# A hybrid attention layer on one core: wider units in the narrow split job, GpSimd's position sums four units ahead, head transposes one tick earlier, and the third query tile beside the first two

## The chip, the cores and the metric

The kernel runs on one core of a Trainium2 chip. The time is the device time of the whole program in microseconds (us); before the change it is 1510.8 us, the median of three runs (1509.91 to 1511.21). The profile is one further execution.

## What is computed

```python
h  = x @ w_in                                    # 512x2048 by 2048x11808, columns q, k, v, z, gates, ...
y_a = (fox(fq, fk, fv, ff + b_f) * silu(fz)) @ w_a   # 8 heads, causal, forget-gate bias
y_b = (nsa(nq, ..., gates) * silu(nz)) @ w_b         # 8 heads, 2 groups; compressed, selected, window branch
out = layer_norm(ALPHA * x + (sigmoid(ga) * y_a + sigmoid(gb) * y_b) @ w_o)
# the compressed branch: blocks of 32 raw keys (values), stride 16, plus a position table, through a two-layer MLP
blocks = raw[:, blk_idx] + pos
k_cmp  = gelu(blocks.reshape(..., 32 * 128) @ w1) @ w2
```

All is float32 and 512 rows long.

## The kernel before

**Units.** The program is one list `units` of pieces of TensorE work. Most need a piece of a weight matrix, which comes by a DMA on SyncE's queue into one of three buffers `wr` (`load`, L159; a chunk is two pieces) and is split into a high and a low part that TensorE multiplies in fp32r: ScalarE copies the high part `wh` (L96), VectorE subtracts for the low part `wl` (L97). A product is three matmuls (`mm3`, L105; `mm_two`, L111). `stream` emits, for unit n, first the split of unit n+3 (`split_w(n + AHEAD)`), then the matmuls of unit n; `wh` and `wl` have four buffers each, so a split can run only when the unit four before it has been multiplied. After the split of a chunk's second half the load of the chunk three further on is issued.

**Ticks.** Attention runs as generators beside the units. Every `tick()` (two 128-row pieces of a projection, six matmuls) advances them by one step: first `active`, then the queue `tq` of second halves of heads (`fox_t`, `nsa_t`), then `sq` of first halves (`fox_s`, `nsa_s`). A FoX head's first half multiplies q by k for four row blocks (`s<-k,q`), takes the exponentials (VectorE L376, ScalarE L378) and normalises the rows (VectorE L387). Its second half transposes them (TensorE L396, out `pt`, two PSUM banks), splits the transposes (`pT`, L96 and L97) and multiplies by v. A transpose of the third step needs the bank whose split was made for the first. All engines work through their instructions in the order emitted.

**Narrow job.** `pairs` computes six column groups of w_in with seven products on half matrices, of eight row tiles of 128 each; T4, T1 and so on name the products. Their right sides are chunks (`wr`) or sums held in `s` and `r`, some made by accumulating DMAs on GpSimd's queue (L979). Five jobs are 512 columns wide; the second, for NSA's values, is 256 wide. One unit is one row tile: six matmuls.

**Position sums.** The compression's first layer is cut in 32 units (`cmp_units`), 16 for keys at heads 1 and 2 and 16 for values at heads 4 and 5, two of them after every two projection units. Each needs four sums of raw keys or values and a position column on GpSimd (L799, `af`), emitted with the unit's split; ScalarE and VectorE then split them (`a<-af`). GpSimd also loads and masks the heads' bias rows (`cbr`, L458, and `cbx`, L462).

**Fill.** `y_fill` multiplies FoX's output by two column groups of w_a beside the last NSA head: eight weight tiles for query tiles 0 and 1, six matmuls each with one tick; then, from the weights kept, tile 2 and tile 3 in units of two weight tiles (`more`). PSUM banks turn over d, d, m.

Of the kernel before, what the change touches and what calls it, by code (L numbers as in the profile page):

```python
# [13 lines left out]
F32R = mybir.dt.float32r  # L14
# [11 lines left out]
H = 8  # L26
# [36 lines left out]
def layer(ctx, tc, x, w_in, b_f, pos_k, pos_v, wk1, wk2, wv1, wv2, w_a, w_b, w_o, ln_g, ln_b, rel, onehot, out):  # L63
# [101 lines left out]
    def split_w(n):  # L165
        while pos["split"] <= min(n, len(units) - 1):
            u = units[pos["split"]]
            pos["split"] += 1
            if "before" in u:
                u["before"]()  # L170
            if "late" in u:
                src = u["late"]()
            elif "chunk" in u:
                w = u.get("width", UW)
                src = chunks[u["chunk"]]["raw"][:, u["half"] * w:(u["half"] + 1) * w]
            else:
                continue
            if "into" in u:
                hi, lo = u["into"]()
            else:  # L180
                hi = base.tile([P, UW], F32R, name="wh", tag="wh", bufs=AHEAD + 1)[:, :src.shape[-1]]
                lo = base.tile([P, UW], F32R, name="wl", tag="wl", bufs=AHEAD + 1)[:, :src.shape[-1]]
            split(hi, lo, src)
            u["w"] = (hi, lo)
            if "prep" in u:
                u["prep"](u)
            if "after" in u:
                u["after"](u)
            if "chunk" in u:
                load(u["chunk"] + 2 + u["half"])  # L190

    def number_chunks():
        for u in units:
# [249 lines left out]
    def fox_t(h, st):  # L443
        key = ("f", h)
        yield from wait_for(("p", key), ("v", key), ("z", key))
        if h < H - 1:
            yield
        yield from take_later("o")
        o = bank("o", 1)
        items = [dict(j=j, p=st["p"], tag=st["tag"], v=vt[key], o=o, first=j == 0, last=j == NT - 1) for j in range(NT)]  # L450
        yield from staged(items, (tr_p, split_p, None, pv))
        gate_out(key, h, o)
        done.add(("t", key))
# [316 lines left out]
    def cmp_units(kv, l00):  # L770

        w = wk1 if kv == "k" else wv1
        at = len(units)

        def pe(u, half):
            l0 = l00 + LB * half
            hi, lo = (t.rearrange("p (l n) -> p l n", l=LB) for t in u["w"])
            a = u["a"]
            n = G * NCMP
            if l0 == 0:  # L780
                assert kv == "k" or ("cmp", "k") in done, "the bank is still in use"
                hid[kv] = bank("m", 1)
            o = hid[kv][:, :CMP_HID]
            for l in range(LB):
                mm_two(o, n, a[:, l], hi[:, l], lo[:, l], l0 + l == 0, l0 + l == CMP_LEN - 1)
            if half:
                tick()
            if l0 + LB == CMP_LEN:
                active.append(cmp_finish(kv))

        def prep(u):
            af = small("af", P, LB * G * NCMP).rearrange("p (l g c) -> p l g c", l=LB, g=G)
            a = pool("fox").tile([P, LB, 2 * G * NCMP], F32R, name="a", tag="a", bufs=AHEAD + 1)
# [7 lines left out]
            split(a[:, :, :n], a[:, :, n:], af.rearrange("p l g c -> p l (g c)"))  # L801
            u["a"] = a

        add_chunk(lambda r: r.rearrange("p (l n) -> p l n", n=CMP_HID),
                  dram(w, l00 * P * CMP_HID, [[CMP_HID, P], [P * CMP_HID, 2 * LB], [1, CMP_HID]]), pe, prep=prep)
        new = units[at:]
        del units[at:]
        return new
# [128 lines left out]
    def pairs(jobs, ops, kh, ent):  # L937
# [24 lines left out]
        def one(j, w, ncols, r0, cols, width, evac):  # L962
# [71 lines left out]
            def out12(width=width, cols=cols, evac=evac):  # L1034
                for i in range(HT):
                    evac(HT + i, cols[0], st[1][i][:, :width], None)


            for op, acc, fresh, quad, after, post in (
                    ("T4", 3, True, (1, 1), first_sum, no_post), ("T1", 1, True, "s", None, keep5),  # L1040
                    ("B11", 0, True, (0, 0), both_sums, keep1), ("T2", 2, True, "s", "sum4", mix),
                    ("B21", 0, False, (1, 0), None, out11), ("T3", 2, False, "r", "rest", out2),
                    ("B22", 1, False, "s", None, out12)):
                for k in range(kh):
                    def pe(u, op=op, acc=acc, fresh=fresh, k=k, post=post, width=width):
                        if fresh and k == 0:
# [10 lines left out]
                    u = {"pe": pe, "width": width}  # L1057
                    if after == "rest":
                        u["after"] = lambda u, k=k, follows=follows: load_rest(k, follows, 1)
                    elif after == "sum4":  # L1060
                        u["after"] = lambda u, k=k: sum4(u, k)
                    elif after is not None and k % 2:
                        u["after"] = lambda u, k=k, after=after: after(k, chunks[u["chunk"]])
                    if quad in ("s", "r"):
                        u["late"] = lambda k=k, quad=quad, width=width: st[quad][:, k, :width]
                    else:
                        u["half"] = k % 2
                        if k % 2 == 0:
                            u["view"] = lambda r, width=width: r[:, :2 * width].rearrange("p (k c) -> p k c", k=2)
                            u["src"] = rows(jobs[j], quad[0] * kh + k, quad[1])  # L1070
                    units.append(u)
            if j == 0:
                units[-7 * kh]["before"] = open_all

        for j, job in enumerate(jobs):
            one(j, *job)
# [199 lines left out]
    def y_fill(n):  # L1276

        st = {}

        def next_bank():  # L1280
            t = fin["turn"] = (fin.get("turn", -1) + 1) % 3
# [8 lines left out]
        def pe(u, kt):  # L1290
            st["w", kt] = u["w"]
            for i in range(2):
                if kt == 0:
                    st[i] = next_bank()
                y_mm(st[i], i, 0, kt, u["w"])
            tick()
            if kt == H - 1:
                gate(0)
                gate(1)

        def more(i, kt):
            def f(u):
                if kt == 0:
# [330 lines left out]
```

## Time and profile before

| | |
|---|---|
| median of three runs | 1510.8 us |
| profiled execution | 1510.6 us |
| its span, first to last instruction | 1508.6 us |
| granted TensorE clock, mean | 0.997 of full |
| TensorE busy | 1488.4 us, 99% |
| VectorE, ScalarE, GpSimd busy | 864.8, 663.0, 221.9 us |

Busy is the time in which an engine has at least one instruction in it; matmuls overlap, so a busy TensorE can still run slowly. The list of waits says for an engine's line what it waited for: total us, times, longest. In a timeline a row is a start in us, a duration, engine, line, operation, out<-in and, in brackets, the idle time before it and what ended it; like rows that touch are merged, so a row can stand for several instructions (x4).

### The profile page before, as it was taken

The page shows a single profiled execution, that of the slowest core. Times are in us where ns is not written, and L with a number is a line of the kernel's source. Part 1 is how long each engine was busy: PE and PEld are TensorE (multiplying, and loading weights), DVE is VectorE, ACT ScalarE, POOL GpSimd, SP SyncE. Part 2 cuts the span into 40 slices and gives each one's busy share as a digit, 9 for nine tenths or more (in the row PEclk, how much of TensorE's full clock was granted, in tenths as well). Part 3 has the DMA queues.
Part 4 walks back from the last instruction along what each step waited for, and adds up shares of the span by engine and source line. Part 5 has one row for each costly group of instructions (what it writes and reads, how often), then busy time and mean ns, then how long its engine had stood idle before and what let it go on. Part 6 is the DMA issues. An engine that isn't in the chain of part 4 may idle for free.

```text
span 1508.6 us, 19701 instructions
## 1 busy us (share of the span) xinstructions
PE 1488.4 (99%) x7081; PEld 1232.6 (82%) x7081; DVE 864.8 (57%) x1721; ACT 663.0 (44%) x1300; POOL 221.9 (15%) x363
## 2 busy tenths in 40 slices
PE   8999999999999999999999999999999999999998
PEld 6788898888888888788787888888887888888886
DVE  4666667676767646645544456646675344444455
ACT  6255665656565535435433344434453222222233
POOL 1211112020101046224230000000000100030001
PEclk9999999999999999999999999999999999999999
DMA  8678578687877564434542332233332433373336
GB/s 228 160 227 194 140 196 196 187 198 192 195 195 190 146 195 147 133 92 129 144 111 77 105 91 71 59 86 93 87 100 85 144 121 122 113 243 98 126 112 167
DMA packets 192176, 214.87 MB, mean 142 GB/s; under 512 B 13024, under 2 KB 127760, under 8 KB 192080
## 3 DMA queue, kind: packets, MB, share of 16 engines
q1 hardware_dynamic: 168688, 159.93, 35.3%
q0 software_dynamic: 23104, 53.18, 16.1%
q8 instruction: 55, 0.90, 0.2%
q10 hardware_dynamic: 288, 0.52, 0.1%
q14 instruction: 41, 0.34, 0.1%
HBM read 195.96 MB, written 21.27 MB: 144 GB/s over the span
## 4 chain that ended last, share of the span: by engine, by line
PE 87%; issue 5%; POOL 3%; DMA 2%; DVE 2%; ACT 1%; SPq 0%; POOLq 0%; ACTq 0%
PE d L105 42%; PE s L105 15%; PE pt L105 9%; PE o L105 9%; PE m L105 8%; POOL af L799 2%; PE pt L396 1%; DMA cbr<-negc_d 1%; DMA wr<-in_w_in_dram 1%; DVE wl L97 1%; PE o L111 0%; POOL cbx L462 0%; PE m L111 0%; PE d L1240 0%; ACT xs L96 0%
## 5 line engine op out<-in xcount | busy, mean ns | idle before, releaser
L97 DVE TENSOR_TENSOR wl<-wr,wh 128x512 fp32r<-128x512 f32 (+1 forms) x476 | 320.9, 681 | 307.4 <-ACT wh L96 298.9
L105 PE MATMUL d<-xs,wh 128*128 128x512 f32 x1504 | 477.5, 398 | 1.0 <-ACT wh L96 0.4
L96 ACT ACTIVATE wh<-wr 128x512 fp32r<-128x512 f32 (+1 forms) x476 | 291.6, 620 | 374.0 <-PE d L105 123.4
L105 PEld LDWEIGHTS d<-xs,wh 128*128 128x128 f32 x1504 | 272.1, 189 | 53.8 <-DVE xs L97 1.6
L105 PE MATMUL d<-xs,wl 128*128 128x512 f32 x752 | 295.4, 393 | 0.0
L105 PEld LDWEIGHTS d<-xs,wl 128*128 128x128 f32 x752 | 141.6, 188 | 32.1 <-DVE wl L97 1.0
L97 DVE TENSOR_TENSOR wl<-s,wh 128x512 fp32r<-128x512 f32 (+1 forms) x144 | 91.3, 646 | 65.9 <-ACT wh L96 65.9
L96 ACT ACTIVATE wh<-s 128x512 fp32r<-128x512 f32 (+1 forms) x144 | 84.0, 595 | 71.2 <-DVE wl L97 53.3
L378 ACT ACTIVATE p<-p,mn 128x128 f32<-128x128 f32 (+3 forms) x96 | 54.1, 564 | 136.6 <-DVE mn L376 136.5
L105 PE MATMUL s<-wh,T 128*128 128x512 f32 (+1 forms) x384 | 112.4, 372 | 0.0
L105 PE MATMUL d<-wh,xs 128*128 128x512 f32 (+1 forms) x336 | 107.0, 382 | 0.2 <-ACT wh L96 0.2
L105 PE MATMUL m<-wh,xs 128*128 128x512 f32 (+1 forms) x256 | 96.1, 379 | 0.0
L105 PE MATMUL o<-wh,xs 128*128 128x512 f32 (+1 forms) x240 | 90.0, 377 | 2.0 <-ACT wh L96 2.0
L105 PEld LDWEIGHTS s<-wh,T 128*128 128x128 f32 x384 | 70.6, 190 | 12.4
L105 PEld LDWEIGHTS d<-wh,xs 128*128 128x128 f32 x336 | 62.2, 188 | 12.1 <-ACT wh L96 0.4
L97 DVE TENSOR_TENSOR pT<-pt,pT 128x512 fp32r<-128x512 f32 (+1 forms) x96 | 46.6, 488 | 43.4 <-ACT pT L96 43.1
L105 PE MATMUL s<-wl,T 128*128 128x512 f32 (+1 forms) x192 | 71.5, 372 | 0.0
L105 PE MATMUL d<-wl,xs 128*128 128x512 f32 (+1 forms) x168 | 64.4, 383 | 0.5
L799 POOL TENSOR_SCALAR af<-raw,posT 128x31 f32<-128x31 f32 x128 | 63.4, 518 | 0.1
L96 ACT ACTIVATE pT<-pt 128x512 fp32r<-128x512 f32 (+1 forms) x96 | 41.2, 431 | 46.8 <-PE pt L396 46.4
L979 POOL DMA_DIRECT2D r<-in_w_in_dram x24 | 28.7, 1197 | 215.8 <-ACT zo L1125 107.8
L105 PE MATMUL pt<-wh,T 128*128 128x512 f32 (+1 forms) x192 | 56.0, 371 | 0.0
(330 smaller groups left out, 2445.8 us busy)
## 6 DMA issues: line engine op xcount, KB each, us to landing
wr<-in_w_in_dram SPq DMA_DIRECT2D x155, 512.0 KB, 3.9
wr<-in_w_o_dram SPq DMA_DIRECT2D x32, 512.0 KB, 3.7
r<-in_w_in_dram SPq DMA_DIRECT2D x20, 512.0 KB, 4.8
r<-in_w_in_dram POOLq DMA_DIRECT2D x20, 512.0 KB, 10.8
s<-in_w_in_dram POOLq DMA_DIRECT2D x20, 512.0 KB, 6.4
wr<-in_w_a_dram SPq DMA_DIRECT2D x16, 512.0 KB, 3.8
wr<-in_w_b_dram SPq DMA_DIRECT2D x16, 512.0 KB, 3.7
sig_d<-zo SPq DMA_DIRECT2D x16, 256.0 KB, 4.5
```

The source lines that it names most:

```text
L96: nc.scalar.activation(hi, src, AF.Copy)
L97: nc.vector.tensor_tensor(lo, src, hi.bitcast(F32), op=ALU.subtract)
L105: nc.tensor.matmul(o, u, v, start=first and n == 0, stop=last and n == 2, **kw)
L378: nc.scalar.activation(row, row, AF.Exp, bias=it["mn"][:, i:i + 1], scale=-1.0, accum_out=it["l"][:, i:i + 1])
L396: nc.tensor.transpose(b[:, (i - j) * P:(i - j + 1) * P], pt[:, OFF[i] + j * P:OFF[i] + (j + 1) * P], ident)
L799: nc.gpsimd.tensor_scalar(af[:, l, g], src, posT[:, po0 + ll:po0 + ll + 1], None, op0=ALU.add)
L979: nc.gpsimd.dma_start(two(n, k), rows(jobs[j], quad[0] * kh + k - 1, quad[1]), accum_op=ALU.add)
```

## The change

In `pairs`, a job of at most 256 columns takes two row tiles in a unit (`per = 2`): one split of 512 columns, twelve matmuls, two ticks. In `cmp_units` the four sums move out of `prep` into `early`, which `split_w` calls when it comes to the unit four before. `fox_t` begins one tick sooner in all heads but the last. In `y_fill` query tile 2 is multiplied beside tiles 0 and 1, four weight tiles behind them, and the units that did this afterwards shrink from four to two.

```diff
@@ split_w
             pos["split"] += 1
+            soon = units[min(pos["split"] + 3, len(units) - 1)]
+            if "early" in soon:
+                soon["early"](soon)
...
-            split(hi, lo, src)
+            if len(src.shape) == 3:
+                split(*(t.rearrange("p (k c) -> p k c", k=src.shape[1]) for t in (hi, lo)), src)
+            else:
+                split(hi, lo, src)
...
-                load(u["chunk"] + 2 + u["half"])
+                load(u["chunk"] + 2 + (1 if u.get("whole") else u["half"]))
@@ fox_t
         yield from wait_for(("p", key), ("v", key), ("z", key))
-        if h < H - 1:
-            yield
         yield from take_later("o")
@@ cmp_units
-        def prep(u):
-            af = small("af", P, LB * G * NCMP).rearrange("p (l g c) -> p l g c", l=LB, g=G)
-            a = pool("fox").tile([P, LB, 2 * G * NCMP], F32R, name="a", tag="a", bufs=AHEAD + 1)
+        def early(u):
+            u["af"] = af = small("af", P, LB * G * NCMP).rearrange("p (l g c) -> p l g c", l=LB, g=G)
...
                     nc.gpsimd.tensor_scalar(af[:, l, g], src, posT[:, po0 + ll:po0 + ll + 1], None, op0=ALU.add)
+        def prep(u):
+            a = pool("fox").tile([P, LB, 2 * G * NCMP], F32R, name="a", tag="a", bufs=AHEAD + 1)
...
@@ pairs
+            per = 2 if 2 * width <= S else 1
...
-                for k in range(kh):
+                for k in range(per - 1, kh, per):
...
-                        hi, lo = u["w"]
-                        for i in range(HT):
-                            a = ops[op]
-                            mm3(st[acc][i][:, :width], (a(0, k, i), a(1, k, i)), (hi, lo), fresh and k == 0, k == kh - 1,
-                                skip_group_check=True)
+                        for v in range(per):
+                            kk, w = k - per + 1 + v, [t[:, v * width:(v + 1) * width] for t in u["w"]]
+                            for i in range(HT):
+                                a = ops[op]
+                                mm3(st[acc][i][:, :width], (a(0, kk, i), a(1, kk, i)), w, fresh and kk == 0, kk == kh - 1,
+                                    skip_group_check=True)
...
-                        tick()
+                        for _ in range(per):
+                            tick()
...
-                        u["late"] = lambda k=k, quad=quad, width=width: st[quad][:, k, :width]
+                        u["late"] = lambda k=k, quad=quad, width=width, per=per: st[quad][:, k - per + 1:k + 1, :width]
@@ y_fill
+        LAG = H // 2
...
+            if kt >= LAG:
+                if kt == LAG:
+                    st[2] = next_bank()
+                y_mm(st[2], 2, 0, kt - LAG, st["w", kt - LAG])
             tick()
...
         for i in range(2, NT):
-            for kt in range(0, H, 2):
+            for kt in range(H - LAG if i == 2 else 0, H, 2):
                 units.append({"pe": more(i, kt)})
```

**ScalarE in the narrow job**, from product T2's splits (`s`) to T3's (`r`); L1010 and L1012 (later L1017 and L1019) copy results that VectorE mixes. Before, then now:

```order
L96 ACTIVATE wh<-s 128x256 x5
L96 ACTIVATE wh<-wr 128x256 x5
L1010 ACTIVATE d<-c_951 128x256
L96 ACTIVATE wh<-wr 128x256
L1012 ACTIVATE c_951<-pt 128x256
L96 ACTIVATE wh<-wr 128x256 x2
```

```order
L96 ACTIVATE wh<-s 128x512
L96 ACTIVATE wh<-wr 128x512 x4
L1017 ACTIVATE d<-c_951 128x256
L1019 ACTIVATE c_951<-pt 128x256
L96 ACTIVATE wh<-r 128x512
```

Eight splits of 256 columns for product B21 have become four of 512, and all stand ahead of the copies.

**GpSimd from the first sums to the masks of the fourth head.** Before, then now:

```order
L318 DMA vT<-v_d 128x4x128
L311 DMA z<-z_d_97 128x512
L799 TENSOR_SCALAR af<-raw,posT 128x31 x12
L458 DMA cbr<-negc_d 128x512
...
L799 TENSOR_SCALAR af<-raw,posT 128x31 x20
...
L799 TENSOR_SCALAR af<-raw,posT 128x31 x8
L458 DMA cbr<-negc_d 128x512
...
L799 TENSOR_SCALAR af<-raw,posT 128x31 x24
```

```order
L803 TENSOR_SCALAR af<-raw,posT 128x31 x8
L325 DMA vT<-v_d 128x4x128
L318 DMA z<-z_d_97 128x512
L803 TENSOR_SCALAR af<-raw,posT 128x31 x12
L463 DMA cbr<-negc_d 128x512
...
L803 TENSOR_SCALAR af<-raw,posT 128x31 x20
...
L803 TENSOR_SCALAR af<-raw,posT 128x31 x8
L463 DMA cbr<-negc_d 128x512
...
L803 TENSOR_SCALAR af<-raw,posT 128x31 x16
```

The sums of two units (x8) have moved ahead of each of GpSimd's other pieces; behind the fourth head's masks 16 are left in place of 24.

**VectorE at FoX head 1**, from the last normalised row to the splits of the transposes; the numbers are those of the buffers' tiles. Before, then now:

```order
L387 TENSOR_SCALAR p_5465<-p_5465,r_5468 128x512
L97 TENSOR_TENSOR wl_5581<-wr_5454,wh_5580 128x512
L97 TENSOR_TENSOR k_5611<-d_5456,k_5611 128x512
L97 TENSOR_TENSOR wl_5615<-wr_5454,wh_5614 128x512
L97 TENSOR_TENSOR wl_5625<-wr_5526,wh_5624 128x512
L97 TENSOR_TENSOR a_5629<-af_5628,a_5629 128x2x62
L97 TENSOR_TENSOR wl_5647<-wr_5526,wh_5646 128x512
L97 TENSOR_TENSOR a_5651<-af_5650,a_5651 128x2x62
L97 TENSOR_TENSOR pT_5667<-pt_5641,pT_5667 128x512
L97 TENSOR_TENSOR pT_5680<-pt_5670,pT_5680 128x384
```

```order
L394 TENSOR_SCALAR p_5363<-p_5363,r_5366 128x512
L97 TENSOR_TENSOR wl_5479<-wr_5352,wh_5478 128x512
L97 TENSOR_TENSOR k_5515<-d_5354,k_5515 128x512
L97 TENSOR_TENSOR wl_5519<-wr_5352,wh_5518 128x512
L97 TENSOR_TENSOR wl_5534<-wr_5424,wh_5533 128x512
L97 TENSOR_TENSOR a_5537<-af_5430,a_5537 128x2x62
L97 TENSOR_TENSOR pT_5544<-pt_5510,pT_5544 128x512
L97 TENSOR_TENSOR wl_5557<-wr_5424,wh_5556 128x512
L97 TENSOR_TENSOR a_5560<-af_5450,a_5560 128x2x62
L97 TENSOR_TENSOR pT_5572<-pt_5547,pT_5572 128x384
```

The first split of a transpose now stands ahead of one pair of weight splits. On TensorE the first four transposes of heads 1 and 4 have moved ahead of the eight short matmuls of a compression unit (L111), those of heads 0, 2, 3, 5 and 6 ahead of six projection matmuls.

## Rows read from the trace of the kernel before

**Rows 1.** TensorE's waits over the whole span: line, waited for: us in total, times, longest.
```profile
PE pt L396 <- DVE pT L97: 4.9, 2, 3.3
PE o L105 <- ACT wh L96: 2.0, 1, 2.0
PE d L105 <- ACT xs L96: 1.0, 2, 0.7
PE d L105 <- ACT wh L96: 0.6, 2, 0.4
PE d L105 <- DVE xs L97: 0.5, 2, 0.2
```
**Rows 2.** The chain that ended last, in order of time (start, us, what), at a wide product, around the narrow job and where the next wide job begins.
```profile
103.12 10.88 PE pt L105 x48
...
179.67 5.75 PE pt L105 x48
...
202.20 6.28 DMA wr<-in_w_in_dram
...
224.87 10.91 PE pt L105 x48
```
**Rows 3.** Stretches of the trace: us, busy (and instructions) of TensorE, its weight loads, VectorE, ScalarE, GpSimd, then the granted TensorE clock, the DMA share and GB/s.
```profile
209.00:212.30 3.30, 3.19 (x14) 2.99 (x15) 2.37 (x6) 2.35 (x8) 0.00 (x0) 0.58 0.46 110
605.20:608.40 3.20, 3.20 (x10) 2.52 (x11) 1.32 (x3) 0.48 (x2) 3.20 (x8) 0.55 0.42 126
718.60:724.00 5.40, 3.85 (x19) 2.83 (x18) 2.71 (x6) 2.35 (x6) 5.36 (x13) 1.00 0.70 224
```
**Rows 4.** Timeline of ScalarE (and one row of VectorE) in the narrow job and just behind it.
```profile
208.57 0.72 ACT L96 ACTIVATE wh<-wr 128x256 fp32r<-128x256 f32 x2 [3.59 <-DMA wr<-in_w_in_dram]
218.91 1.41 ACT L1125 ACTIVATE c<-c 128x256 f32<-128x256 f32 x4 [0.82 <-DVE c L1023]
223.41 1.42 DVE L97 TENSOR_TENSOR wl<-wr,wh 128x512 fp32r<-128x512 f32 x2 [0.50 <-ACT wh L96]
231.74 0.64 ACT L96 ACTIVATE wh<-s 128x512 fp32r<-128x512 f32 x1 [0.36 <-PE pt L105]
```
**Rows 5.** DMA issues from 165 to 240 us: count, KB each, median us from issue to landing.
```profile
wr<-in_w_in_dram SPq DMA_DIRECT2D x9, 256.0 KB, 2.8
s<-in_w_in_dram POOLq DMA_DIRECT2D x4, 256.0 KB, 6.0
```
**Rows 6.** Timeline of GpSimd and of ScalarE's waits for its sums at heads 1 and 4.
```profile
596.67 2.68 POOL L462 TENSOR_SCALAR_AFFINE_SELECT cbx<-cbr 128x128 f32<-128x128 f32 x4 [3.55 <-DMA cbr<-negc_d]
601.76 0.31 ACT L96 ACTIVATE a<-af 128x124 fp32r<-128x124 f32 x1 [2.99 <-POOL af L799]
713.29 5.66 POOL L799 TENSOR_SCALAR af<-raw,posT 128x31 f32<-128x31 f32 x8
718.98 0.31 ACT L96 ACTIVATE a<-af 128x124 fp32r<-128x124 f32 x1 [2.09 <-POOL af L799]
```
**Rows 7.** Timeline of TensorE and VectorE at heads 0, 1, 2 and 4: the last normalised row, the transposes, the splits.
```profile
566.88 0.49 DVE L387 TENSOR_SCALAR p<-p,r 128x512 f32<-128x512 f32 x1
569.86 0.60 PE L396 MATMUL pt<-ident,p 128*128 128x128 f32 x4
...
596.93 0.28 PE L111 MATMUL m<-wh,a 128*124 128x256 f32 x1
597.48 0.49 DVE L387 TENSOR_SCALAR p<-p,r 128x512 f32<-128x512 f32 x1
598.00 0.60 PE L396 MATMUL pt<-ident,p 128*128 128x128 f32 x4
599.40 1.32 DVE L97 TENSOR_TENSOR wl<-wr,wh 128x512 fp32r<-128x512 f32 x2
605.18 0.44 PE L396 MATMUL pt<-ident,p 128*128 128x128 f32 x2 [3.32 <-DVE pT L97]
...
633.09 0.62 PE L105 MATMUL d<-xs,wh 128*128 128x512 f32 x2
633.61 0.49 DVE L387 TENSOR_SCALAR p<-p,r 128x512 f32<-128x512 f32 x1
...
714.15 0.51 DVE L387 TENSOR_SCALAR p<-p,r 128x512 f32<-128x512 f32 x1
714.34 0.28 PE L111 MATMUL m<-wh,a 128*124 128x256 f32 x1
720.55 0.44 PE L396 MATMUL pt<-ident,p 128*128 128x128 f32 x2 [1.55 <-DVE pT L97]
```
**Rows 8.** VectorE's weight subtractions beside GpSimd's sums (566.3 to 577.8 us) and without any (640 to 668 us): count, busy us, mean ns.
```profile
L97 DVE TENSOR_TENSOR wl<-wr,wh 128x512 fp32r<-128x512 f32 x8 | 5.8, 735 | 2.5 <-ACT wh L96 2.4
...
L97 DVE TENSOR_TENSOR wl<-wr,wh 128x512 fp32r<-128x512 f32 x9 | 6.2, 689 | 7.4 <-ACT wh L96 6.2 <-PE s L105 1.2
```
**Rows 9.** Timeline of the fill at its sixth weight tile, and the gates (L1225) of query tiles 0 and 1.
```profile
1141.88 0.69 DVE L97 TENSOR_TENSOR xs<-wr,xs 128x512 fp32r<-128x512 f32 x1 [1.41 <-ACT xs L96]
1141.90 0.49 PE L105 MATMUL d<-xs 128*128 128x512 f32 x1 [0.71 <-ACT xs L96]
1142.62 1.43 PE L105 MATMUL d<-xs 128*128 128x512 f32 x5 [0.23 <-DVE xs L97]
1147.31 1.28 DVE L1225 TENSOR_TENSOR om<-d,om 128x512 f32<-128x512 f32 x2
```

More of the change, by code (lines that the diff above doesn't have):

```diff
@@ L180, in split_w @@
             else:
-                hi = base.tile([P, UW], F32R, name="wh", tag="wh", bufs=AHEAD + 1)[:, :src.shape[-1]]
-                lo = base.tile([P, UW], F32R, name="wl", tag="wl", bufs=AHEAD + 1)[:, :src.shape[-1]]
-            split(hi, lo, src)
+                w = u.get("width", UW)
+                hi = base.tile([P, UW], F32R, name="wh", tag="wh", bufs=AHEAD + 1)[:, :w]
+                lo = base.tile([P, UW], F32R, name="wl", tag="wl", bufs=AHEAD + 1)[:, :w]
+            if len(src.shape) == 3:
+                split(*(t.rearrange("p (k c) -> p k c", k=src.shape[1]) for t in (hi, lo)), src)
+            else:
+                split(hi, lo, src)
             u["w"] = (hi, lo)
@@ L799, in prep @@
                     nc.gpsimd.tensor_scalar(af[:, l, g], src, posT[:, po0 + ll:po0 + ll + 1], None, op0=ALU.add)
+        def prep(u):
+            a = pool("fox").tile([P, LB, 2 * G * NCMP], F32R, name="a", tag="a", bufs=AHEAD + 1)
             n = G * NCMP
-            split(a[:, :, :n], a[:, :, n:], af.rearrange("p l g c -> p l (g c)"))
+            split(a[:, :, :n], a[:, :, n:], u["af"].rearrange("p l g c -> p l (g c)"))
             u["a"] = a
         add_chunk(lambda r: r.rearrange("p (l n) -> p l n", n=CMP_HID),
-                  dram(w, l00 * P * CMP_HID, [[CMP_HID, P], [P * CMP_HID, 2 * LB], [1, CMP_HID]]), pe, prep=prep)
+                  dram(w, l00 * P * CMP_HID, [[CMP_HID, P], [P * CMP_HID, 2 * LB], [1, CMP_HID]]), pe, prep=prep, early=early)
         new = units[at:]
@@ L1043, in one, with pe @@
                     ("B22", 1, False, "s", None, out12)):
-                for k in range(kh):
-                    def pe(u, op=op, acc=acc, fresh=fresh, k=k, post=post, width=width):
-                        if fresh and k == 0:
+                for k in range(per - 1, kh, per):
+                    def pe(u, op=op, acc=acc, fresh=fresh, k=k, post=post, width=width, per=per):
+                        if fresh and k == per - 1:
                             st[acc] = x_bank(acc)
-                        hi, lo = u["w"]
-                        for i in range(HT):
-                            a = ops[op]
-                            mm3(st[acc][i][:, :width], (a(0, k, i), a(1, k, i)), (hi, lo), fresh and k == 0, k == kh - 1,
-                                skip_group_check=True)
+                        for v in range(per):
[4 more added lines that the diff above has]
+                                    skip_group_check=True)
                         if k == kh - 1:
                             post()
-                        tick()
-                    u = {"pe": pe, "width": width}
+                        for _ in range(per):
+                            tick()
+                    u = {"pe": pe, "width": per * width}
                     if after == "rest":
@@ L1064, in one @@
                     if quad in ("s", "r"):
-                        u["late"] = lambda k=k, quad=quad, width=width: st[quad][:, k, :width]
+                        u["late"] = lambda k=k, quad=quad, width=width, per=per: st[quad][:, k - per + 1:k + 1, :width]
                     else:
-                        u["half"] = k % 2
-                        if k % 2 == 0:
+                        u["half"] = 0 if per == 2 else k % 2
+                        u["whole"] = per == 2
+                        if u["half"] == 0:
                             u["view"] = lambda r, width=width: r[:, :2 * width].rearrange("p (k c) -> p k c", k=2)
-                            u["src"] = rows(jobs[j], quad[0] * kh + k, quad[1])
+                            u["src"] = rows(jobs[j], quad[0] * kh + k - k % 2, quad[1])
                     units.append(u)
             if j == 0:
-                units[-7 * kh]["before"] = open_all
+                units[-7 * kh // per]["before"] = open_all
         for j, job in enumerate(jobs):
@@ L1302, in f @@
             def f(u):
-                if kt == 0:
+                if i == NT - 1 and kt == 0:
                     st[i] = next_bank()
```

## The prediction

> **What bounds the kernel now.** I read the page first, then TensorE's waits, the chain that ended last, and the timelines where that chain leaves TensorE. TensorE is busy for 1488.4 of 1508.6 us, and its waits for other engines sum to a few us [rows 1]. So no engine's total matters; a gain can only be a stall of TensorE that goes, and a loss one that comes. The reader is to see in the list of waits that four places hold nearly all of it: transposes that wait for VectorE (two places, 4.9 us), the output bank `o` that waits for a ScalarE copy (one, 2.0 us), and `d` products that wait for `xs` (0.7 us and less) [rows 1].
>
> The list understates two of them. In the chain a wide product of 48 matmuls takes 10.88 us, so six matmuls, one tick, take 1.36 us; a narrow one takes 5.75 us, and seven would take 40.25, but the narrow job runs from 179.67 to 224.87, 45.20 us: 4.95 are lost where the list has 2.0 [rows 2]. The stretches show why: behind the 2.0 us wait the granted clock is 0.58 of full for 3.3 us, mostly the 1.2 GHz level in place of 2.4, and behind the longest transpose wait (3.32 us) it is 0.55 for 3.2 us; behind the one of 1.55 us it stays at 1.00 [rows 3, 7]. An idle of 2 us or more thus cost 3.3 x 0.42 = 1.4 us on top, one of 1.55 nothing.
>
> **Term 1, the narrow job.** ScalarE sat for 3.59 us before 208.57 until a weight chunk had landed [rows 4]; its load was issued at 202.20 and took 6.28 us, where nine such loads have a median of 2.8, since four accumulating transfers of 6.0 us each run then [rows 2, 5]. The load is issued when the second half of the chunk three before it has been split. A unit was 5.75/8 = 0.72 us, and that half was split three units before its own matmuls, 1.44 us before the chunk's first. Now a unit is 1.44 us and the chunk is split as a whole 4.32 us before its first matmul, 2.88 earlier. One split of 512 columns ends about 0.64 + 0.71 = 1.35 us after its start (high part, low part), one of 256 about 0.42 + 0.43 in the same shares (0.36 a copy back to back), so 0.5 of it is lost: the load goes out 2.4 us earlier against TensorE. The accumulating transfers move by the same amount, so its 6.28 us should stay. Of the 2.4 us, 0.3 go again because the first matmul behind a landing waits for a copy of 0.64 in place of 0.36 [rows 4]. 2.1 against a wait of 2.02: the wait goes, narrowly, and the slow stretch with it; if 0.5 us of it stayed, the clock would still hold. The job's second loss, where ScalarE's four copies of 1.41 us [rows 4] stand ahead of the last splits, has 4.32 us of lead in place of 2.16 and goes as well. Bounds: all 4.95; or, where a landing sets the pace, 0.3 lost. I take **4.8**, near the upper end, because both waits are shorter than the lead that is added.
>
> **Term 2, the sums.** At head 1 GpSimd masks the bias rows from 596.67, having waited 3.55 us for their transfer, and the sums queued behind came so late that ScalarE waited 2.99 us; at head 4 the same cost 2.09 [rows 6]. The split of the transposes stands behind on both engines, so TensorE waited 3.32 and 1.55 us for a bank [rows 7]. Now the sums that stand behind those masks are those of units four further on. Between lie two projection units and two compression units, 2 x 2.72 + 2 x 0.96 = 7.4 us (a compression unit is eight matmuls of 256 columns, 0.12 each as in the narrow job's 5.75/48). At head 4 eight sums of 5.66 us that began at 713.29 [rows 6] will be wanted from about 724, not 717: the wait goes. What is moved past costs nothing that is waited for: the transfers of v and z at head 1 and two `cbr` loads go out about eight sums, 5.66 us at most, later on GpSimd's queue, and the masks behind those loads waited for VectorE longer than that or are wanted a head later.
>
> What is late next at head 1 is VectorE itself. From the two subtractions at 599.40 (1.32 us) [rows 7] it goes on with `a` (some 0.3), then the transposes' split (512 columns, 0.69 [rows 8]): done at about 601.7. On TensorE's new schedule (below) the bank is wanted at about 597.97 + 0.96 for the compression unit + 1.9 for a step's transposes and six matmuls = 600.85: 0.85 us of wait in place of 3.32 and its slow stretch of 1.4. Bounds: none, or the old 4.8.
>
> **Term 3, the tick.** Heads 0 to 6 transpose one step sooner. The fourth of the first transposes needs the last normalised row. Head 0 has 569.86 - 567.37 = 2.49 us to spare and gives up 1.36: nothing [rows 7]; heads 3, 5 and 6 have more. At head 1 the row ends at 597.97, 0.03 before the transposes; their new place is ahead of a compression unit, 596.93, and three transposes need no wait and take some 0.27 us of it (four take 0.60 with the last one's tail), so TensorE stands for 597.97 - 596.93 - 0.27 = 0.77. At head 2 the place is 633.09 and the row ends at 634.10: 0.74. At head 4, 714.34 and 714.66: 0.05 [rows 7]. None is near 2 us. In return the first split of the transposes stands ahead of one pair of weight splits on VectorE, and that is already in the 0.85. So head 1 costs 0.77 + 0.85 = 1.6 in place of 4.8, a gain of **3.2**; head 4 costs 0.05 plus about 0.4 for its two banks by the same reckoning in place of 1.55, a gain of **1.1**; head 2 loses **0.75**.
>
> Here a rule speaks against moving the sums. Eight subtractions beside them took 735 ns on average, nine without them 689 [rows 8]: 46 ns each, and three lie ahead of the transposes' split at head 1, 0.14 us, which they bore before too. The Trainium skill, SBUF — State Buffer, Who interferes with whom, says that a VectorE instruction with two SBUF inputs and a GpSimd instruction that reads SBUF exclude each other, the later one waiting for the whole of the earlier. By the rows I add nothing; by that rule each subtraction could wait for a whole sum.
>
> **Term 4, the fill.** TensorE waits 0.71 us for the high part of weight tile 5 and 0.23 more for the low part, which VectorE finishes at 1142.57 [rows 9]. The three matmuls of tile 2 that now stand before it are 0.68 us of work; TensorE arrives at 1141.87 and still waits for the low part. Gain **0.7**; at least 0, at most 0.94. The fourth query tile now begins two units, 2.7 us, after the eighth weight tile in place of four; it needs the bank of tile 0, whose gate ran as that tile ended (1147.31, both gates 1.28 us) [rows 9]: covered by 1.4 us. Four ticks fewer only spread attention's last steps into the second fill.
>
> **The sum.** 4.8 + 3.2 + 1.1 - 0.75 + 0.7 = 9.05 us from the profiled execution's 1510.6 (span 1508.6, 2.0 around it): 1501.5. The median, 1510.8, is 0.2 above that execution, within the runs' own spread, and I add nothing for it. If all lost time went and none came, 4.95 + 4.8 + 1.55 + 0.94 = 12.2: 1498.4.
>
> **The rivals.**
> - *The chunk still lands late.* If the earlier loads meet the transfers harder and land 2 us later, wait and slow stretch stay and only the second loss goes, 0.8: 1501.5 + 4.0 = 1505.5. For it: the margin is 0.1. Against: a wait has to reach about 2 us before the clock adds to it.
> - *VectorE holds head 1 over 2 us*, so that the clock falls there as before: 1501.5 + 3.2 = 1504.7. For it: VectorE has no idle time there from 597.88 on. Against: 0.85 by its own rows.
> - *The exclusive port.* A sum takes 5.66/8 = 0.71 us [rows 6]; three subtractions that each wait for one make head 1's split 2.1 us later, the idle 2.95, and the clock adds 1.4: 1501.5 + 3.5 = 1505.0. The 735 ns speak against it. This is the rule of the Trainium skill's SBUF — State Buffer, Who interferes with whom, taken in full.
> - *Both first rivals together*: 1508.7, no change that can be told.
> - *Slower: the sooner transposes outrun the rows.* If at heads 0, 1, 2 and 4 TensorE arrives over 2 us before the last normalised row, each costs what head 1 cost, 4.8: 19.2, against 4.8 + 0.7 + 4.8 + 1.55 = 11.85 won: 1518.0. It decides from 2 us at each head; the rows give 0.77, 0.74, 0.05 and none.
> - *The change does nothing in one part*, as where the narrow units' loads were already early: inside the first rival.
>
> **How the numbers follow.** Forecast 0.64, late chunk 0.13, VectorE 0.10, port 0.04, both 0.04, slower 0.05. About 0.2%, 3.0 us, is what a measurement here can tell from no change: faster is below 1507.8. Faster 0.91, same 0.04, slower 0.05. The range goes from 1498.0 (every loss gone, with some of the runs' spread) to 1505.6, over the single rivals at 1505.5 or less.
>
> **What would show it.** The narrow job from its first to its last matmul near 40.4 us with the clock at full; no wait of ScalarE for a chunk near its third product, or one that TensorE does not feel. ScalarE's waits for `af` (L799, now L803) gone. TensorE's waits at the transposes: two of 0.5 to 0.9 us for normalised rows at heads 1 and 2, about 1 us or less for a bank, and no clock below 0.9 there. In the fill a wait for VectorE alone. Any idle of TensorE over 2 us in these places would make the prediction wrong.

## The result, and the profile after

The changed kernel takes 1502.1 us, the median of six runs (1500.79 to 1502.9), against 1511.01 (1509.91 to 1512.5) for the kernel before beside it: ratio 0.9939, 95% interval 0.9927 to 0.9952. The forecast was 1501.5. The profiled execution took 1501.35 us, with a span of 1499.3 and a mean clock of 0.999.

TensorE's waits in the changed kernel (line, waited for: us in total, times, longest), to be held against [rows 1]:

```profile
PE pt L403 <- DVE p L394: 1.2, 2, 0.6
PE pt L403 <- DVE pT L97: 0.8, 2, 0.4
...
PE d L105 <- DVE xs L97: 0.5, 2, 0.2
PE d L105 <- ACT wh L96: 0.4, 1, 0.4
...
PE d L105 <- ACT xs L96: 0.3, 1, 0.3
```

The 4.9 us of transposes behind VectorE are 0.8, `o` behind ScalarE's copies is gone, and a wait is new: two transposes now wait for normalised rows (`p`).

The chain that ended last, at the narrow job (start, us, what), against [rows 2]:

```profile
179.62 5.75 PE pt L105 x48
...
208.49 5.99 PE s L105 x48
214.47 5.76 PE d L105 x48
220.23 10.91 PE pt L105 x48
```

From 179.62 to 220.23 are 40.61 us where 45.20 stood, and the load that stood in the chain there is gone from it. Stretches of the changed kernel with the columns of [rows 3], the narrow job and head 1:

```profile
179.62:219.95 40.33, 40.33 (x337) 40.13 (x335) 25.54 (x44) 21.68 (x44) 8.27 (x7) 1.00 0.92 230
...
593.00:599.00 6.00, 5.30 (x29) 4.31 (x30) 5.18 (x12) 4.05 (x10) 6.00 (x12) 1.00 0.64 182
```

The clock, the third number from the right, is at full in both. ScalarE still waits for the chunk of [rows 4], but in the list above TensorE no longer waits for it. Timeline of SyncE's queue and ScalarE there:

```profile
199.82 0.37 SPq L159 DMA_DIRECT2D wr<-in_w_in_dram  x1
205.36 0.63 ACT L96 ACTIVATE wh<-wr 128x512 fp32r<-128x512 f32 x1 [3.40 <-DMA wr<-in_w_in_dram]
```

TensorE's timeline at FoX heads 1, 2 and 4: each head's first scores (`s<-k,q`, 128x128), and every transpose that waits:

```profile
579.78 0.45 PE L105 MATMUL s<-k,q 128*128 128x128 f32 x3
...
592.31 0.49 PE L403 MATMUL pt<-ident,p 128*128 128x128 f32 x3
593.31 0.33 PE L403 MATMUL pt<-ident,p 128*128 128x128 f32 x1 [0.51 <-DVE p L394]
...
596.68 0.41 PE L403 MATMUL pt<-ident,p 128*128 128x128 f32 x2 [0.39 <-DVE pT L97]
...
611.89 0.44 PE L105 MATMUL s<-k,q 128*128 128x128 f32 x3
...
625.51 0.33 PE L403 MATMUL pt<-ident,p 128*128 128x128 f32 x1 [0.64 <-DVE p L394]
...
654.60 0.45 PE L105 MATMUL s<-k,q 128*128 128x128 f32 x3
...
694.01 0.45 PE L105 MATMUL s<-k,q 128*128 128x128 f32 x3
...
710.30 0.41 PE L403 MATMUL pt<-ident,p 128*128 128x128 f32 x2 [0.38 <-DVE pT L97]
...
739.52 0.45 PE L105 MATMUL s<-k,q 128*128 128x128 f32 x3
```

Three transposes run, the fourth waits for its row: the shape that the forecast named. From one head's first scores to the next head's, head 1 takes 32.11 us (611.89 - 579.78), head 2 42.71, head 4 45.51; in the trace before, by the same starts, 36.19, 41.81 and 46.63:

```profile
584.41 0.45 PE L105 MATMUL s<-k,q 128*128 128x128 f32 x3
...
620.60 0.44 PE L105 MATMUL s<-k,q 128*128 128x128 f32 x3
...
662.41 0.45 PE L105 MATMUL s<-k,q 128*128 128x128 f32 x3
...
701.81 0.45 PE L105 MATMUL s<-k,q 128*128 128x128 f32 x3
...
748.44 0.45 PE L105 MATMUL s<-k,q 128*128 128x128 f32 x3
```

ScalarE in the changed kernel at head 1, against [rows 6]:

```profile
594.62 0.29 ACT L96 ACTIVATE a<-af 128x124 fp32r<-128x124 f32 x1
594.81 0.58 ACT L96 ACTIVATE pT<-pt 128x512 fp32r<-128x512 f32 x1
...
595.81 0.30 ACT L96 ACTIVATE a<-af 128x124 fp32r<-128x124 f32 x1
```

No split of a sum waits for GpSimd. VectorE's weight subtractions and GpSimd's sums from 592 to 599 us (count, busy us, mean ns), against [rows 8]:

```profile
L97 DVE TENSOR_TENSOR wl<-wr,wh 128x512 fp32r<-128x512 f32 x6 | 4.3, 724 | 2.2 <-ACT wh L96 2.2
...
L803 POOL TENSOR_SCALAR af<-raw,posT 128x31 f32<-128x31 f32 x13 | 8.0, 643 | 0.0
```

VectorE's subtractions are hardly longer for the 13 sums beside them, 724 ns in the mean. The sums are: 643 ns in the mean, where one that VectorE leaves alone takes 0.39 us. Timeline of VectorE (`pt` lies in PSUM, so the last split has one input in SBUF, the subtractions have two) and GpSimd, where a row of x2 holds two instructions:

```profile
594.42 1.28 DVE L97 TENSOR_TENSOR wl<-wr,wh 128x512 fp32r<-128x512 f32 x2
595.86 0.68 DVE L97 TENSOR_TENSOR pT<-pt,pT 128x512 fp32r<-128x512 f32 x1
...
594.50 1.37 POOL L803 TENSOR_SCALAR af<-raw,posT 128x31 f32<-128x31 f32 x1
595.86 0.39 POOL L803 TENSOR_SCALAR af<-raw,posT 128x31 f32<-128x31 f32 x1
```

A sum that begins inside a weight subtraction ends only behind it. Over the whole trace 28 such sums take 0.96 us in the mean (23 in the trace before: 0.93), and 39 that begin and end with VectorE idle take 0.39 (before: 46, 0.40).

And the fill at its sixth weight tile, against [rows 9]:

```profile
1132.91 0.50 PE L105 MATMUL d<-xs 128*128 128x512 f32 x1
1133.63 1.45 PE L105 MATMUL d<-xs 128*128 128x512 f32 x5 [0.23 <-DVE xs L97]
```

The wait for ScalarE is gone, that for VectorE stayed, as the forecast had it.

### The profile page after: what moved, and what is told of

Read it like the earlier page. It is cut to its first block, busy times and chain, and to the rows that moved or that the text cites. A ratio compares the mean times of both kernels' runs of the same rounds, so it can differ in the third digit from the quotient of the medians.

```text
span 1499.3 us, 19624 instructions
## 1 busy us (share of the span) xinstructions
PE 1484.9 (99%) x7081; PEld 1229.9 (82%) x7081; DVE 861.4 (57%) x1693; ACT 656.0 (44%) x1272; POOL 223.3 (15%) x363
## 4 chain that ended last, share of the span: by engine, by line
PE 94%; DVE 2%; ACT 1%; DMA 1%; issue 1%; SPq 0%; ACTq 0%; DVEq 0%
PE d L105 47%; PE s L105 16%; PE o L105 9%; PE pt L105 9%; PE m L105 8%; PE pt L403 2%; DVE wl L97 1%; PE m L111 1%; PE o L111 1%; DMA xn<-in_x_dram 0%; ACT p L385 0%; PE d L1251 0%; DVE p L383 0%; ACT xs L96 0%; DMA vT<-nv_d 0%
## 5 line engine op out<-in xcount | busy, mean ns | idle before, releaser
L97 DVE TENSOR_TENSOR wl<-wr,wh 128x512 fp32r<-128x512 f32 x464 | 319.9, 695 | 313.5 <-ACT wh L96 305.0
L96 ACT ACTIVATE wh<-wr 128x512 fp32r<-128x512 f32 x464 | 289.1, 629 | 382.9 <-PE d L105 128.0
L97 DVE TENSOR_TENSOR wl<-s,wh 128x512 fp32r<-128x512 f32 x132 | 89.7, 691 | 64.7 <-ACT wh L96 64.7
L96 ACT ACTIVATE wh<-s 128x512 fp32r<-128x512 f32 x132 | 81.5, 629 | 70.1 <-DVE wl L97 55.4
```

What stands on the lines that cost most here:

```text
L96: nc.scalar.activation(hi, src, AF.Copy)
L97: nc.vector.tensor_tensor(lo, src, hi.bitcast(F32), op=ALU.subtract)
```

## The experiments

The kernels were run five to eleven times each, in three groups with the kernel before beside each group: 1511.28, 1511.48 and 1510.64 us. Ratios are 95% intervals. In the tables "narrow" is the narrow job from its first to its last matmul by their starts, and a head's length is that between first scores, as above.

**Group 1: each part alone, in the kernel before.**

| | us | ratio to before | narrow | head 1 | head 2 | head 4 |
|---|---|---|---|---|---|---|
| before (trace) | 1511.28 | | 45.09 | 36.19 | 41.81 | 46.63 |
| changed (trace) | 1502.1 | 0.9939 | 40.49 | 32.11 | 42.71 | 45.51 |
| narrow job only | 1507.99 | 0.9966 to 0.9985 | 40.34 | 37.27 | 41.82 | 46.64 |
| early sums only | 1505.13 | 0.9945 to 0.9973 | 45.31 | 31.86 | 41.80 | 44.91 |
| sooner transposes only | 1506.65 | 0.9960 to 0.9981 | 44.68 | 32.09 | 42.60 | 45.50 |
| fill only | 1509.54 | 0.9986 to 1.0003 | 44.89 | 34.63 | 41.81 | 46.63 |

*The narrow job alone*: the edits of `pairs` and `split_w`, nothing else.

```diff
+            per = 2 if 2 * width <= S else 1
-                for k in range(kh):
+                for k in range(per - 1, kh, per):
```

> The kernel before with only the narrow job's units of two row tiles. Theory of the lead (each stall pays for itself): the narrow job takes 40.6 us as in the changed kernel in place of 45.2, everything behind it is shifted by that and nothing else moves; about 4.6 us faster. Rival, the gain is shared: with the rest of the change left out, the later stalls at the heads grow or the clock falls elsewhere, and the whole gains under 2.5 us.

In the trace the job gets 4.75 us shorter; the median time only 3.3, between the two theories, and the eleven runs spread from 1503.58 to 1510.09. In the profiled execution head 1 came out 1.1 us longer (see the hardware below). For the job itself the part is shown.

*The early sums alone*: `early` in `cmp_units` and its call in `split_w`.

```diff
-        def prep(u):
+        def early(u):
```

> The kernel before with only the position sums four units ahead; the transposes begin as before. Theory that the sums carry this part: ScalarE's waits for the sums go; at head 1 VectorE still splits one pair of weights ahead of the transposes, so TensorE waits about 0.8 us for a bank, at head 4 about nothing, and head 2 loses nothing: about 5.5 us faster, more than the sums and the tick together (about 4.2 by the changed kernel's trace). Rival, the tick carries it: without the sooner transposes head 1 still idles about 2 us or more and the clock falls, gain under 3 us.

6.15 us: 4.33 at head 1, 1.72 at head 4, nothing lost at head 2. TensorE's timeline at head 1 shows what is left, one bank wait:

```profile
602.69 0.44 PE L403 MATMUL pt<-ident,p 128*128 128x128 f32 x2 [0.57 <-DVE pT L97]
```

*The sooner transposes alone.*

```diff
-        if h < H - 1:
-            yield
```

> The kernel before with only the sooner transposes of heads 0 to 6. Theory that the sums carry this part: head 1 waits about 0.5 us for its last row and still 2.4 us for the bank, since the first late sum stands ahead of it; head 4 loses its 1.55 us wait because the second late sum now stands behind the split; head 2 loses 0.75: in all 0 to 1.5 us faster. Rival, the tick carries it: 3 us or more faster.

This expectation was wrong: 4.6 us, and head 1 as short as with all parts. ScalarE's timeline of this kernel at head 1 says why:

```profile
599.02 0.29 ACT L96 ACTIVATE a<-af 128x124 fp32r<-128x124 f32 x1
599.21 0.58 ACT L96 ACTIVATE pT<-pt 128x512 fp32r<-128x512 f32 x1
...
601.83 0.31 ACT L96 ACTIVATE a<-af 128x124 fp32r<-128x124 f32 x1 [1.51 <-POOL af L797]
602.04 0.74 ACT L96 ACTIVATE pT<-pt 128x384 fp32r<-128x384 f32 x2
```

The sum is still late and ScalarE still waits for it, but the transposes' first copy (`pT`, 599.21) now stands ahead of the waiting split and not behind it. Either part takes the stall away; so with both, one of them buys nothing at head 1.

*The fill alone*: `LAG`, as in the diff ahead.

```diff
+            if kt >= LAG:
+                y_mm(st[2], 2, 0, kt - LAG, st["w", kt - LAG])
```

> The kernel before with only query tile 2 beside tiles 0 and 1 in the fill. Theory: the wait of 0.71 us for the high part of weight tile 5 shrinks to 0.0 to 0.1 us, the one for the low part (0.23) stays, 0.7 us faster, hardly to be told in the times and to be read from the fill's length (52.3 us in place of 53.0). Rival: a wait for the bank of query tile 0 or 2 takes its place and the fill's length stays at 53.0 or grows.

In the trace the fill, from its first matmul to the first behind it, takes 52.37 in place of 53.01 us, 0.64; the time's interval reaches past no change. Right in the trace, too small for the runs.

**Group 2: parts taken back from the changed kernel, and what the narrow job gains by.**

| | us | ratio to before | narrow | head 1 | head 2 | head 4 |
|---|---|---|---|---|---|---|
| old tick put back | 1501.83 | 0.9926 to 0.9951 | 40.81 | 31.84 | 41.81 | 44.90 |
| sums not early | 1503.58 | 0.9933 to 0.9960 | 41.90 | 32.07 | 42.64 | 45.48 |
| narrow splits in halves | 1502.21 | 0.9931 to 0.9956 | 40.20 | 32.09 | 42.71 | 45.52 |
| narrow chunk asked for later | 1502.62 | 0.9933 to 0.9958 | 41.00 | 32.09 | 42.72 | 45.51 |

```diff
+        if h < H - 1:
+            yield
```

> The changed kernel with the old wait of one tick ahead of the heads' transposes put back (heads 0 to 4); narrow job, early sums and fill stay as changed. Theory A (early sums and sooner transposes each remove the same stall of head 1, so either is enough; the sooner transposes then only move the transposes closer to the rows they wait for): the scores of head 2 to head 3 take 41.8 us again instead of 42.7 and head 4 to head 5 44.9 instead of 45.5, head 1 to head 2 31.9 instead of 32.1; 1.7 us in all: 1500.3 us, 0.9989 of the changed kernel, and the waits of pt on p are gone. Theory B (each part removes a share of its own, the terms add up): head 1 takes some 33.5 us, a wait of pt on pT of over 1 us is back, and the time is 1503 to 1504 us.

By the trace theory A holds at every head, 1.78 us over heads 1, 2 and 4, and the wait on `p` is gone. The median gained 0.3 only; the run was repeated (group 3).

```diff
-        def early(u):
+        def prep(u):
```

> The changed kernel with GpSimd's sums put back behind their unit's split (not four units ahead); the transposes stay sooner, narrow job and fill as changed. Theory A (substitutes): 1501.5 to 1502.5 us, no difference from the changed kernel; head 1 to head 2 32.1 us, the first wait on the sums on ScalarE is back (1.5 us or more) but falls behind the copy of pT that TensorE wants. Theory B (terms add up): head 1 to head 2 over 33.5 us, the time 1503.5 to 1505.

The heads are as theory A says: 32.07, and the split of a sum that waits falls behind the copy that TensorE wants. The time is not: 1.1 to 1.5 us more, in the range of theory B. In the profiled execution the heads have no part in it, and 1.4 us stand in the narrow job, in instructions that this edit doesn't touch. Timeline of SyncE's queue, ScalarE and TensorE in this kernel's narrow job and at head 1:

```profile
199.92 0.37 SPq L159 DMA_DIRECT2D wr<-in_w_in_dram  x1
206.94 0.63 ACT L96 ACTIVATE wh<-wr 128x512 fp32r<-128x512 f32 x1 [4.89 <-DMA wr<-in_w_in_dram]
207.62 0.39 PE L105 MATMUL o<-wh,xs 128*128 128x256 f32 x1 [0.48 <-ACT wh L96]
208.35 0.39 PE L105 MATMUL o<-wl,xs 128*128 128x256 f32 x1 [0.34 <-DVE wl L97]
...
596.88 0.58 ACT L96 ACTIVATE pT<-pt 128x512 fp32r<-128x512 f32 x1
...
599.49 0.31 ACT L96 ACTIVATE a<-af 128x124 fp32r<-128x124 f32 x1 [1.52 <-POOL af L804]
```

The same load landed 7.0 us after its issue here, 5.5 in the changed kernel's trace, and TensorE waited. The heads of the profiled executions carry the verdict on the sums; the job's 1.4 us are those of the profiled execution. How much of them the other runs had is not shown, so what made the median longer stays open.

```diff
-                split(*(t.rearrange("p (k c) -> p k c", k=src.shape[1]) for t in (hi, lo)), src)
+                for r in range(src.shape[1]):
+                    c = slice(r * src.shape[2], (r + 1) * src.shape[2])
+                    split(hi[:, c], lo[:, c], src[:, r])
```

(and the same for sums held in `s` and `r`)

> The changed kernel with the narrow job's whole units as they are, but each of its splits of 512 columns issued as two of 256 (ScalarE, VectorE: twice the instructions for the same columns, the order of the units and the loads kept). Theory A (the narrow job gains by the lead of a unit of two row tiles over TensorE): the narrow job still takes 40.6 to 41.2 us from its first scores to its last transpose, and the time is within 0.7 us of the changed kernel. Theory B (it gains because half as many instructions go through the two engines, each with its fixed cost): ScalarE's and VectorE's 256-column instructions come late again, TensorE waits for xs or wh 1 to 4 us in the job, which takes 42 to 45 us; the time 1503.5 to 1506.

40.20, in the trace, with twice the instructions: the gain is the lead of a unit of two row tiles, not the smaller number of instructions.

```diff
-                load(u["chunk"] + 2 + (1 if u.get("whole") else u["half"]))
+                load(u["chunk"] + 2 + (0 if u.get("whole") else u["half"]))
```

> The changed kernel, where a narrow unit's split starts the load of the chunk one further back: it asks for the chunk two ahead, which its predecessor asked for already in the changed kernel, so that each narrow chunk starts some 5.8 us later (one unit of 48 matmuls; less where ScalarE waits for a chunk anyway). In the changed kernel the chunk of the fourth unit landed some 1 us before TensorE needed its split, not 0.1 us as the sum had it. Theory A (the load's start sets it): TensorE waits 3 to 5 us in all in the narrow job, with a stretch at about 0.58 of the clock behind it: the job takes 44 to 47 us and the time is 1505 to 1509 us. Theory B (the chunk is a prefetch with slack to spare, the gain is from wider units alone): the job stays within 0.5 us of 40.6, the time within 0.7 us of the changed kernel.

This tells the theories apart less than meant, since the edit hardly moved this load: 20.29 us after the job's first matmul, 20.36 in the changed kernel. Its buffer came free no later, and nothing but the loads of earlier chunks stood shortly before it on SyncE's queue. The next load the edit did move: behind ten transfers of `r` and `nv_d` on that queue it went out 38.1 us after the first matmul in place of 27.3, too late to bear on this job. What the executions show together is the landing of the job's last chunk against the job:

| | asked for after job's start | landed after that | narrow job |
|---|---|---|---|
| narrow job only | 20.29 | 5.47 | 40.34 |
| changed | 20.36 | 5.54 | 40.49 |
| changed, again (group 3) | 20.28 | 5.67 | 40.55 |
| old tick put back | 20.50 | 5.71 | 40.81 |
| old tick put back, again | 20.30 | 5.98 | 40.87 |
| narrow chunk asked for later | 20.29 | 6.12 | 41.00 |
| sums not early | 20.29 | 7.02 | 41.90 |
| narrow splits in halves | 20.15 | 5.97 | 40.20 |

(landed: ScalarE's start on it.) In the first seven the job ends 14.6 us after the landing, each time within 0.02 us: the later it lands, the longer the job. By that line a job of 40.19 us, the shortest seen, needs a landing at about 5.3 us (an estimate), so that every one of the seven was late, by 0.15 to 1.7 us. The kernel with the splits in halves stands apart: it lands late and loses nothing. There the first half is split sooner behind the landing; that this is the reason is not shown, and it is one trace.

**Group 3: the two leads followed up.** The changed kernel again, with the old tick, with larger chunks, and with both.

| | us | ratio to before | narrow | head 1 | head 2 | head 4 |
|---|---|---|---|---|---|---|
| changed, again | 1502.45 | 0.9930 to 0.9956 | 40.55 | 32.09 | 42.70 | 45.51 |
| old tick, again | 1501.59 | 0.9923 to 0.9951 | 40.87 | 31.94 | 41.81 | 44.90 |
| larger chunks | 1500.93 | 0.9926 to 0.9952 | 40.19 | 32.11 | 42.72 | 45.52 |
| larger chunks, old tick | 1499.69 | 0.9915 to 0.9941 | 40.19 | 31.92 | 41.81 | 44.90 |

The changed kernel again, without an edit:

> The changed kernel once more, beside the three below on the same chip: 1501.5 to 1502.7 us. In the narrow job its twelfth chunk (the last of its fifth product) is asked for some 20.4 us behind the job's start and lands 5.5 to 7.0 us later, as that load did in four executions of the same instructions; TensorE waits for its split 0 to 0.8 us, and the job takes 40.4 to 41.9 us.

The old tick again, the edit of group 2:

> The changed kernel with the old tick ahead of the heads' transposes, again, now beside the changed kernel on one chip. Theory A (the sooner transposes cost 1.7 us by the profile: head 2 0.9, head 4 0.6, head 1 0.25, and nothing gives it back): 1.7 us less than the changed kernel, 1500.4 us. Theory B (the same work, only its waits lie elsewhere, or what the start of a run adds is as large): within 0.5 us of the changed kernel.

0.9 us less, between the two theories. Over both groups ten runs against the changed kernel's eleven differ by 0.56 us in the mean (95%, by drawing the runs anew: 1.3 less to 0.1 more). The traces say 1.65 to 1.78 in the three pairs; these runs can't hold it, for the first narrow matmul alone starts at 179.39 to 181.09 us in the traces, after the same instructions. The third pair, the last two rows of the table, does: 1.6 us less in the mean (0.9 to 2.4).

```diff
-                        u["half"] = 0 if per == 2 else k % 2
-                        u["whole"] = per == 2
+                        u["half"] = k // per % 2
...
-                            u["src"] = rows(jobs[j], quad[0] * kh + k - k % 2, quad[1])
+                            u["src"] = rows(jobs[j], quad[0] * kh + k - k % 2, quad[1], 2 * per)
```

(and the view and the sums take the half that `k` names)

> The changed kernel, where a chunk of the narrow job holds four row tiles (512 KB, the whole buffer) and feeds two whole units, in place of two row tiles (256 KB, half of a buffer) and one unit: six loads for twelve, over the same three buffers, so that a chunk is asked for when the second unit of the chunk three before it has been split and its sum made. Theory A (the narrow job's remaining wait is the last chunk's late landing, since only three units are loaded ahead): the last chunk is asked for at some 190 us instead of 199.8, no split of the fifth product waits for a load, the job takes 40.2 to 40.5 us, and the time is 0.3 to 0.8 us under the changed kernel's. Theory B (a chunk twice as large lands later, behind the accumulating loads, and the split waits for it elsewhere): the job takes 41 to 43 us and the time is 0.5 to 2 us over the changed kernel's.

Theory A, by the trace; the runs differ from the changed kernel's beside them by 0.6 us in the mean (1.5 less to 0.4 more). Timeline of SyncE's queue and ScalarE in that kernel:

```profile
190.85 0.38 SPq L159 DMA_DIRECT2D wr<-in_w_in_dram  x1
...
201.78 0.63 ACT L96 ACTIVATE wh<-wr 128x512 fp32r<-128x512 f32 x1 [0.81 <-PE s L105]
203.22 0.64 ACT L96 ACTIVATE wh<-wr 128x512 fp32r<-128x512 f32 x1 [0.81 <-PE s L105]
```

The last chunk is asked for at 190.85 and its splits wait for TensorE, for a buffer, not for a DMA; the job takes 40.19 us in both kernels that have it, where nothing but matmuls is left (seven products of 5.76 are 40.3).

The larger chunks and the old tick together, both edits above:

> Chunks of four row tiles in the narrow job and the old tick put back, with the early sums, the wider units and the fill as changed: by the two theories A above 2.0 to 2.5 us under the changed kernel, 1499.6 to 1500.1 us; by the theories B 1501.5 to 1503.

1499.69 us, the fastest version here: under the changed kernel beside it by 2.2 us in the mean (1.2 to 3.2). TensorE's timeline at heads 1 and 2 shows the one wait left:

```profile
598.30 0.44 PE L403 MATMUL pt<-ident,p 128*128 128x128 f32 x2 [0.89 <-DVE pT L97]
...
626.66 0.66 PE L403 MATMUL pt<-ident,p 128*128 128x128 f32 x4
```

## Why the prediction was right, step by step

| term | forecast | trace |
|---|---|---|
| 1, narrow job | 4.8 | 4.6 |
| 2 and 3, head 1 | 3.2 | 4.1 |
| 3, head 4 | 1.1 | 1.1 |
| 3, head 2 | -0.75 | -0.9 |
| 4, fill | 0.7 | 0.7 |
| sum | 9.05 | 9.6 (span 9.3) |

**Term 1** held in its mechanism; its size came out in part by luck. The load goes out 2.3 us earlier against the job's start (20.20 after the first product's row in the chain, 22.53 before), where 2.4 was worked out. The margin was not there: the sum left 0.1 us at a landing of 6.28, but with 6.12 the job lost 0.8 against the 40.19 that it takes without such a wait, with 7.02 it lost 1.7, and by the line of the table 6.28 would cost 1.0 (an estimate). The profiled execution drew 5.54 and lost 0.3. Most of those 0.3 do not stand at the chunk's own matmuls, where the forecast looked, but in the next product (5.99 us in the chain, 5.76 the one behind it), whose splits of `r` come behind the late one on ScalarE and VectorE. So the rival of the late chunk happens, in small, in all seven; it never came near the 4.0 us of its price, since a landing 0.7 us later than forecast left waits of 0.48 and 0.34 us and cost 1.4 us against the changed kernel's trace.

**Head 1** was mis-sized in the two waits that were to come: 0.51 for the row and 0.39 for the bank, not 0.77 and 0.85. The old idle of 3.32 less these 0.90 is 2.4; the slow clock, 1.4 to 1.6 in that execution, is the rest. What the forecast did not see is that Terms 2 and 3 are one gain there, not two: [rows 6] put the lateness on the sums, and the order of VectorE's instructions, ahead of the prediction, already showed the transposes' split passing one pair with a sum in it. That was read as a help of the tick to a gain that the sums make. The sooner transposes alone make it too.

**Heads 2 and 4**: the row wait at head 2 came (0.64; 0.9 in all), none at head 4. Taken together the tick costs: without it heads 1, 2 and 4 are 0.2, 0.9 and 0.6 us shorter. The forecast's -0.75 was thus a loss without a return; by the traces, and by the runs with the larger chunks, the changed kernel would be better without this part.

**The rivals.** VectorE did not hold head 1 over 2 us (0.39). The price of the exclusive port did not come: with the sums beside them six subtractions took 724 ns each, and the bank wait is shorter than forecast. The two engines do hold each other up all the same, and GpSimd pays: a sum that begins inside a subtraction takes 0.96 us in place of 0.39. The Trainium skill, SBUF — State Buffer, Who interferes with whom, has a VectorE instruction with two SBUF inputs contend with a GpSimd instruction that reads SBUF; the trace agrees. The other way round little was seen: of 61 subtractions that begin beside a running sum, in both traces, 60 took 0.68 to 0.80 us (one 0.96), where the means without are 0.68 and 0.69. The prediction took a sum at 0.71 us, from eight beside subtractions [rows 6]; that is a sum with its waits in it. Eight alone would take some 3.1 us in place of 5.66 (an estimate, 8 x 0.39), so these waits are part of why the sums were late at head 4; no run took them away. The transposes did outrun the rows at heads 1 and 2, by 0.5 and 0.6 us, far from the 2 us of the slower rival.

## What to carry to other kernels

Before two edits are priced as two gains, follow the one instruction that is late: an edit that makes its input earlier and one that moves it ahead of the waiting instruction buy the same stall once, and the second then only costs. The load that set the narrow job went out when its buffer came free, and asking for it one unit later changed nothing; a load that was put behind other transfers on the queue did go out later. A missing margin against a landing time shows up as scatter between executions, and half as many chunks of twice the size removed it here without a byte more. Look at both engines before two are said to overlap freely: VectorE's mean hid a wait that GpSimd's showed. In a kernel whose TensorE is busy 99%, read gains of under 2 us from the stage's own length in the trace: medians of five runs mostly did not hold them.

## What was unexpected of the hardware

The price of a stall through the clock is not fixed by its length. The prediction took about 2 us of idle as the point at which the clock adds 1.4 us. In the kernel with the sooner transposes alone, TensorE's timeline has a wait of 1.64 us in the narrow job:

```profile
208.94 0.38 PE L105 MATMUL o<-wh,xs 128*128 128x256 f32 x1 [1.64 <-ACT wh L96]
```

and the stretch behind it in the same kernel is at the 1.2 GHz level (clock 0.50):

```profile
210.60:213.90 3.30, 3.30 (x18) 3.30 (x17) 2.00 (x5) 2.13 (x8) 0.00 (x0) 0.50 0.79 173
```

while head 4's wait of 1.55 us before the change cost no clock [rows 3, 7]. And the stall of head 1, whose instructions and wait (3.32 to 3.34 us) are the same in three traces, was followed by 3.2 us at 0.55 in the kernel before [rows 3], by nothing in the kernel with the fill alone, and in the kernel with the narrow job alone its last microsecond lay in a stretch of 6.4 us at half clock. The stretches, of the fill alone and then of the narrow job alone:

```profile
606.00:609.20 3.20, 3.20 (x16) 2.62 (x17) 1.56 (x4) 0.78 (x3) 3.20 (x8) 1.00 0.45 135
```

```profile
601.10:607.50 6.40, 5.40 (x15) 4.24 (x16) 2.66 (x6) 1.77 (x5) 6.29 (x16) 0.50 0.30 82
```

Head 1's lengths follow: 36.19, 34.63 and 37.27 us. So the slow clock's 1.4 us of head 1 in the sum was a draw, 0 to about 2.6 in these three, and that the sum had the right size there is luck in part; what makes it so is open.
